# Even spacing of filler blocks in the seven-product pairs, a tied convolution product, and two transposes set a step apart, in a Mamba-2 layer

## The chip, the cores and the metric

The kernel runs on one core of a Trainium2 chip. The metric is the device time of one execution in microseconds, taken over several executions, and the median is used. One further execution was recorded by the hardware profiler; every duration, wait and clock below is from that one.

Engine names: PE is the matrix engine, DVE the vector engine, ACT the scalar engine, POOL the general engine, SP the engine that issues most DMAs.

## The reference

Four steps are chained on a residual stream of 256 tokens by 2048 columns in fp32: multi-head latent attention, a squared-ReLU MLP, a Mamba-2 mixer, a second MLP. Only the Mamba-2 mixer is touched here:

```python
def ssm_mixer(h, w_in, conv_w, conv_b, dt_bias, a_log, d_skip, norm_g, w_out):
    zxbcdt = h @ w_in                            # 2048 -> 4096 z, 4096 x, 1024 B, 1024 C, 64 dt
    z, xbc, dt = jnp.split(zxbcdt, [...], axis=-1)
    xbc = jax.nn.silu(causal_depthwise_conv(xbc, conv_w, conv_b))     # 4 taps along the tokens
    ...
    y = ssd_chunked_scan(xs, dt, a, b_in, c_in)  # 64 heads in 8 groups
    y = y + d_skip[..., None] * xs
    y = y.reshape(B, S, SSM_D_INNER) * jax.nn.silu(z)
    y = y.reshape(B, S, SSM_GROUPS, 512)
    y = y * lax.rsqrt(jnp.mean(y * y, axis=-1, keepdims=True) + RMS_EPS)
    return (y.reshape(B, S, SSM_D_INNER) * norm_g) @ w_out
```

## The kernel before

**Arithmetic.** Each fp32 operand is split into a high word that the PE takes at full rate and a remainder. A product of activations and weights is then three matmuls: high by high, low by high, high by low. Weights come in pieces of 128x1024 (512 KB), called units: one DMA into a raw buffer (`wraw`, or `wrx` where the unit needs a longer life), an ACT copy that gives the high word `wh` (L102), a DVE subtraction that gives the remainder `wl` (L103). `wh` and `wl` have four buffers each, so a unit can be split only when PE has used up the unit four before it. The raw buffers are a ring too: a load starts when the last reader of the buffer before it is done.

**Stage.** The touched stage lies between about 1018 and 1526 us. It first makes B and C (columns "B 0" and "C 0"), the dt chain, and block x4; then the x columns of groups 0 to 3 in two *pairs*, p0 and p1, of two groups each; then a list of steps `SSM_ORDER`: convolutions ("v"), the second halves of B and C, z blocks ("z", with the gating of y) and output blocks ("o").

**A pair** computes a 2x2 block product by seven products instead of eight (`ssm_seven`). The products are M1, N7, N5, N6, N4, M2, N3, each cut into four depths d = 0..3. A piece is written here as N70 (product N7, depth 0): six matmuls, 1.36 us on PE. Some of them need weights that are sums of two quarters; DVE forms these in place (L183, `b22`, `b12` and `b11`): in front of N7 `b22 = b12 + b22`, in front of N5 `b12 = b11 + b12`, in front of N6 `b11 = b11 + b22`. N4 uses `b11` again after a DMA has added a quarter to it.

**Fillers.** A product piece of 1.36 us on PE needs up to two DVE operations of 1.22 us, so PE would outrun DVE. Between the pieces therefore stand fillers: eighths of the x blocks of groups 5, 6 and 7 (x5/0 is the first eighth of x5), twelve matmuls, 2.72 us on PE, one DVE operation. `woven(p)` writes the order: it balances a sum of PE time against a sum of DVE time, with earliest times for N4, M2 and N3. `SSM_FILLERS` says which eighths belong to which pair. The order that it gives for the end of p0, the start of p1, and the end of p1:

```text
p0: ... N63 x6/3 M20 M21 M22 M23 N30 N31 N32 N43 N33
p1: x6/4 x6/5 M10 N70 x6/6 N50 x6/7 N60 M11 N71 x7/0 N51 x7/1 N61 x7/2 N40 M12 N72 x7/3 N52 ...
p1: ... N53 x7/6 N63 x7/7 N42 M20 M21 M22 M23 N30 N31 N43 N32 N33
```

**Ticks.** Work beside the matmuls is put into a queue by `later(n, fn)`: it runs at the n-th coming tick. Outside the pairs every two units of a block (24 matmuls, 5.4 us) end with a tick; inside them `spend` counts 5.4 us of PE time as one.

**Order on the engines.** PE runs in program order. On the other engines a list scheduler sets the order when the kernel is built, except where `issue_after` ties an instruction behind another one: `behind("last_lo")` ties DVE work behind the remainder (L103) that was written last, `behind("last_load")` ties loads behind the last weight load on SP.

**Convolution of x** (`x_conv(g, wait)`). The x columns were written to DRAM (`put_x`, L1326 and L1327) and are read back four times, shifted by 0 to 3 tokens: `xtm` (L1353) and three `tap` tiles (L1344); each has its weights `cw` (L1340). DVE multiplies and adds them: `mult` takes the unshifted rows and tap 2, `tapped(1)` tap 1 (L1359 the product, L1356 the sum), `total` the rest. Group 0's is called in p1 when N5 and N6 are both complete (`free`, at N63).

**Gating of y** (`z_block(g)`). When y of group g is ready, `gate` makes for each token half t = 0, 1 a gated and normed 128x512 tile, and three ticks later `transposes` turns it on PE into a bank of PSUM (L322 and L324), which ACT and DVE then split into the k4 tiles that the output blocks read (L299, L300). The transposes use the pool `sm`, which has two banks. `cb_group` (L1307, L1308) uses the same pool, and its matmuls stand right ahead of the transposes at groups 3 and 4.

Of the kernel before, what the change touches and what calls it, by code (L numbers as in the profile page):

```python
# [214 lines left out]
class Trunk:  # L215
# [959 lines left out]
    def ssm_body(self, sp, dp, gain, later):  # L1175
# [15 lines left out]
        hq, cms, ready, gated, batch, sp2 = [], [], {}, set(), [], []  # L1191
# [143 lines left out]
        def x_conv(g, wait):  # L1335
            cw, tap, xts = {}, {}, []

            def weight(k):
                cw[k] = sp.tile([P, 512], F32, tag="cw", name=f"cw{g}_{k}", bufs=3)
                nc.sync.dma_start(cw[k], d["cwx"][g][:, k * 512:(k + 1) * 512])  # L1340

            def load(k):
                tap[k] = self.flow.pools["rx"].tile([P, 2, 512], F32, tag="rx", name=f"tap{g}_{k}")
                nc.sync.dma_start(tap[k], x_rows(g, 0, 2, k))  # L1344

            def fetch(*todo):
                with behind("last_load"):
                    for fn in todo:
                        fn()

            def whole():
                xts.append(xn.tile([P, 2, 512], F32, tag="xn", name=f"xtm{g}"))
                nc.sync.dma_start(xts[0], x_rows(g, 0, 2))  # L1353

            both = lambda k: cw[k].unsqueeze(1).to_broadcast([P, 2, 512])
            plus = lambda v: nc.vector.tensor_tensor(xts[0], xts[0], v, ALU.add)  # L1356

            def tapped(k):
                nc.vector.tensor_tensor(tap[k], tap[k], both(k), ALU.mult)  # L1359
                plus(tap[k])  # L1360

            def mult():
                with behind("last_lo"):
                    nc.vector.tensor_tensor(xts[0], xts[0], both(3), ALU.mult)
                    tapped(2)
                fetch(lambda: weight(0), lambda: weight(4))

            def total():
                with behind("last_lo"):
                    plus(both(4))  # L1370
                    tapped(0)

            def tanh():
                tap[3] = self.flow.pools["rx"].tile([P, 2, 512], F32, tag="rx", name=f"th{g}")
                with behind("last"):
                    nc.scalar.activation(tap[3], xts[0], AF.Tanh, scale=0.5)

            def silu():
                with behind("last_lo"):
                    nc.vector.scalar_tensor_tensor(xts[0], tap[3], 1.0, xts[0], ALU.add, ALU.mult)  # L1380

            def ahead():
                x = xg[g] = [xts[0][:, t] for t in range(2)]
                heads_of = lambda v: v.rearrange("p (h f) -> p h f", h=8)
                spread = lambda v: v[:, 8 * g:8 * g + 8].unsqueeze(2).to_broadcast([P, 8, 64])
                xw = self.scratch()
                nc.gpsimd.tensor_tensor(heads_of(xw), heads_of(x[0]), spread(edge[:, 0]), ALU.mult)

                def across():
                    b = self.bank(False)  # L1390
                    nc.tensor.matmul(b, cb[g][:, P:256], xw, start=True, stop=True)
                    far[g] = sp2[0].tile([P, 512], F32, tag="far", name=f"far{g}", bufs=2)
                    nc.vector.tensor_tensor(heads_of(far[g]), heads_of(b), spread(edge[:, 1]), ALU.mult)

                self.later(2, across)

            self.later(wait, lambda: fetch(whole, lambda: weight(3), lambda: load(2), lambda: weight(2), lambda: load(1)))
            self.later(wait + 1, lambda: fetch(lambda: weight(1), lambda: load(0)))
            self.later(wait + 3, mult)
            self.later(wait + 4, lambda: tapped(1))  # L1400
            self.later(wait + 4, lambda: cb_group(g))
            self.later(wait + 5, lambda: (total(), hq.extend((g, i) for i in range(8))))
            self.later(wait + 6, tanh)
            self.later(wait + 7, lambda: (silu(), ahead()))
# [61 lines left out]
        yT = [None] * GROUPS  # L1466

        def z_block(g):
            accs = self.block([("si", "z", g, q) for q in range(4)], xT)
            ssq = self.stat(2)  # L1470
            ws = []
            for t in range(2):
                w = self.scratch()
                nc.scalar.activation(w, accs[t], AF.Tanh, scale=rsh[t])
                nc.vector.scalar_tensor_tensor(w, w, 1.0, accs[t], ALU.add, ALU.mult)
                ws.append(w)
            yT[g] = (self.ktile(self.k4), self.ktile(self.k4))

            def gate():
                if self.ticks < ready.get(g, self.ticks + 1):  # L1480
                    self.later(0, gate)
                    return
                ng = self.gain_tile(d["sng"][g], nc.gpsimd)
                for t in range(2):
                    x = xg[g][t]
                    nc.gpsimd.tensor_tensor(x, ws[t], x, ALU.mult)
                    self.square_sum(x, ssq[:, t:t + 1], scale=rs[t])
                rr = self.rsqrt(ssq, 2, 512, 4 * EPS)
                r = self.stat(2)
                nc.vector.tensor_tensor(r, rr, rs2, ALU.mult)  # L1490
                for t in range(2):
                    nc.vector.scalar_tensor_tensor(ws[t], xg[g][t], r[:, t:t + 1], ng, ALU.mult, ALU.mult)
                    w = self.words(ws[t], 4 - t)
                    self.later(3, lambda t=t, w=w: self.transposes(w, yT[g][0], yT[g][1], t, False))
                self.later(3, lambda: gated.add(g))

            self.later(0, gate)

# [4 lines left out]
        out = {}  # L1503
# [12 lines left out]
        with ExitStack() as first:  # L1516
            sp1 = first.enter_context(self.tc.tile_pool(name="ssm1", bufs=1, reuse_waits="tile"))
            sums, steps = self.sums_of_tokens(sp1, xn)
            for n, fn in zip(SUMS_AT, steps):
                self.later(n, fn)  # L1520
            bc_block("B", 0)
            dt_block()
            bc_block("C", 0)
            x_block(4)
            for p in range(2):
                self.ssm_seven(sums, p, filler, lambda p, j, t, src, dst: put_x(2 * p + j, t, src, dst),
                               (lambda: x_conv(0, 0)) if p else None)
        sp2.append(later.enter_context(self.tc.tile_pool(name="ssm2", bufs=1, reuse_waits="tile")))
        self.pump = pump

        for step in SSM_ORDER:
# [12 lines left out]
            else:  # L1544
# [12 lines left out]
HEAD_BACKLOG = 4  # L1557
TINY = 1.2e-38
SUMS_AT = (5, 8, 11)
SSM_FILLERS = [[("x", 5, o) for o in range(8)] + [("x", 6, o) for o in range(4)],  # L1560
               [("x", 6, o) for o in range(4, 8)] + [("x", 7, o) for o in range(8)]]
SSM_ORDER = ["v1+3", "B1", "C1", "v2+1", "z0", "z1", "v3", "z2", "z3", "v4", "o0a", "o0b", "v5", "z4", "z5", "v6", "o1a", "v7+1",
             "o1b", "z6", "z7", "o2a", "o2b", "o3"]

# [1 line left out]
def woven(p):  # L1566


    main = [(n, d) for d in range(4) for n in ("M1", "N7", "N5", "N6")]
    late = [("N4", d) for d in range(4)]  # L1570
    second = [("M2", d) for d in range(4)] + [("N3", d) for d in range(4)]
    units = list(SSM_FILLERS[p])
    pe = 28 * 1.36 + 2.72 * len(units)
    ve = 40 * 1.22 + 1.22 * len(units) + 5 * 0.68
    t = work = 0.0
    rest, done, out = -9.0, {}, []

    def ready(n, d):
        if n == "N4":
            return t >= done.get(("N6", d), 1e9) + 12  # L1580
        if n == "M2":
            return t >= done.get(("M1", 3), 1e9) + 7
        if n == "N3":
            return t >= max(done.get((q, 3), 1e9) for q in ("N5", "N6")) + 7
        return True

    while main or late or second or units:
        op = next((q for q in (late, main, second) if q and ready(*q[0])), None)
        if units and t >= rest and (op is None or work > t * ve / pe - 2):
            b = units.pop(0)  # L1590
            out.append(b)
            t, work = t + 2.72, work + 1.22
            if b[2] == 7:
                rest = t + 4
        else:
            if op is None:
                op = late or second
            n, d = op.pop(0)
            out.append(("s", p, n, d))
            t, work = t + 1.36, work + {"M1": 1.22, "N4": 1.22, "M2": 1.22, "N3": 1.22}.get(n, 2.44)  # L1600
            done[n, d] = t
    return out

# [220 lines left out]
```

## Time and profile before

| | |
|---|---|
| median of 3 runs | 2300.14 us (2298.83 to 2300.56) |
| the profiled execution | 2302.01 us, its span 2300.2 us, mean granted clock 0.997 |
| PE busy | 2277.0 us, 99% of the span |
| DVE, ACT, POOL busy | 1961.4 (85%), 1443.1 (63%), 279.7 us (12%) |
| the stage, 1022 to 1180 us (both pairs) | PE busy 149.8 of 158 us |
| the stage, 1180 to 1526 us | PE busy 340.3 of 346 us |
| PE's waits from 1010 to 1530 us | 8.1 us for `wl`, 4.7 us for a bank at L322, 0.9 us elsewhere |

The profiled execution is 1.9 us above the median, and 1.8 us of it lie around the span. A line of the timeline reads: start and duration in us, engine, line, operation, what it writes and reads, shapes, count, and in brackets how long the engine stood idle before it and what it waited for. A line of the waits reads: who waits, for whom, us in total, times, longest. In a table of windows each engine has its busy time and number of instructions, then come the granted clock of PE (1.00 is full speed), the DMA engines' share, and GB/s. A matmul's printed duration overlaps the next one's, so distances between starts are what count.

### The profile page before, as it was taken

The numbers are of one execution on the slowest core, as the hardware profiler recorded it, in microseconds if no ns is written. First come the engines' busy times: TensorE is split into PE (matmuls) and PEld (weight loads), VectorE is DVE, ScalarE is ACT, GpSimd is POOL, SyncE is SP. The second block draws the span as 40 slices with busy tenths as digits, with TensorE's granted clock in tenths as the row PEclk, the third lists the DMA queues.
The fourth block names the chain that finished last, engine by engine and source line by source line (L and its number), as shares of the span: only waits on it lengthen the run. The fifth ranks groups of instructions, "written<-read, shape, count | busy, mean of one in ns | idle before, by whom it ended". The sixth has DMA issues, their size and how long they took to land.

```text
span 2300.2 us, 30834 instructions
## 1 busy us (share of the span) xinstructions
PE 2277.0 (99%) x10881; PEld 1884.4 (82%) x10881; DVE 1961.4 (85%) x2257; ACT 1443.1 (63%) x2044; POOL 279.7 (12%) x339
## 2 busy tenths in 40 slices
PE   9999999999999999999999999999999999999999
PEld 7888888888888888888778887788888887888887
DVE  7786698998899897887879998876989989989985
ACT  7775466566666666566567676564666665666663
POOL 1440000000000000100002532230000000000000
PEclk9999999999999999999999999999999999999999
DMA  8545688888888877768798888866688888888875
GB/s 314 171 153 166 210 232 265 257 257 258 271 256 258 275 226 244 246 186 274 231 340 289 285 284 295 303 213 221 204 260 247 266 268 247 257 271 250 264 230 164
DMA packets 176026, 569.74 MB, mean 248 GB/s; under 512 B 20192, under 2 KB 29344, under 8 KB 175872
## 3 DMA queue, kind: packets, MB, share of 16 engines
q1 hardware_dynamic: 147808, 498.24, 65.0%
q0 software_dynamic: 16320, 56.88, 11.6%
q10 hardware_dynamic: 11744, 12.66, 1.7%
q8 instruction: 85, 1.39, 0.2%
q14 instruction: 69, 0.57, 0.1%
HBM read 542.23 MB, written 6.41 MB: 239 GB/s over the span
## 4 chain that ended last, share of the span: by engine, by line
PE 89%; DVE 5%; DMA 3%; ACT 1%; issue 1%; POOL 0%; ACTq 0%; DVEq 0%; SPq 0%
PE acc L339 10%; PE acc L340 10%; PE acc L343 10%; PE yp L619 9%; PE yp L618 9%; PE yp L617 9%; PE st L618 7%; PE st L619 7%; PE st L617 7%; DVE wl L103 3%; DMA wraw<-mi 1%; PE st L1162 1%; PE yp L339 1%; PE yp L340 1%; PE yp L343 1%
## 5 line engine op out<-in xcount | busy, mean ns | idle before, releaser
L102 ACT ACTIVATE wh<-wraw 128x1024 fp32r<-128x1024 f32 (+1 forms) x818 | 857.8, 1053 | 541.6 <-PE acc L340 189.9
L103 DVE TENSOR_TENSOR wl<-wraw,wh 128x1024 fp32r<-128x1024 f32 (+1 forms) x818 | 986.1, 1224 | 171.4 <-ACT wh L102 162.6
L617 PE MATMUL yp<-wh,k 128*128 128x512 f32 x896 | 349.3, 390 | 0.0
L619 PE MATMUL yp<-wh,k 128*128 128x512 f32 x896 | 348.8, 389 | 0.0
L618 PE MATMUL yp<-wl,k 128*128 128x512 f32 x896 | 348.6, 389 | 0.0
L102 ACT ACTIVATE wh<-wrx 128x1024 fp32r<-128x1024 f32 x192 | 203.0, 1059 | 169.5 <-PE yp L619 98.4
L103 DVE TENSOR_TENSOR wl<-wrx,wh 128x1024 fp32r<-128x1024 f32 x192 | 233.0, 1221 | 39.8 <-ACT wh L102 39.2
L339 PE MATMUL acc<-wh,k 128*128 128x512 f32 x496 | 196.7, 397 | 0.3 <-ACT k L299 0.3
L618 PEld LDWEIGHTS yp<-wl,k 128*128 128x128 f32 x896 | 168.2, 188 | 35.0
L619 PEld LDWEIGHTS yp<-wh,k 128*128 128x128 f32 x896 | 168.2, 188 | 34.9
L617 PEld LDWEIGHTS yp<-wh,k 128*128 128x128 f32 x896 | 168.3, 188 | 34.8
L340 PE MATMUL acc<-wh,k 128*128 128x512 f32 x496 | 193.7, 391 | 0.8 <-DVE k L300 0.8
L339 PE MATMUL acc<-wh,xt 128*128 128x512 f32 x480 | 191.5, 399 | 0.3 <-ACT wh L102 0.2
L340 PE MATMUL acc<-wh,xt 128*128 128x512 f32 x480 | 187.6, 391 | 0.1
L617 PE MATMUL st<-wh,xt 128*128 128x512 f32 x448 | 177.7, 397 | 0.0
L619 PE MATMUL st<-wh,xt 128*128 128x512 f32 x448 | 174.9, 390 | 0.0
L618 PE MATMUL st<-wl,xt 128*128 128x512 f32 x448 | 174.7, 390 | 0.0
L199 POOL DMA_DIRECT2D wrx<-mi x56 | 49.0, 875 | 723.5 <-DVE wl L103 513.0
L617 PE MATMUL st<-wh,sN 128*128 128x512 f32 x336 | 133.1, 396 | 0.8 <-ACT wh L102 0.8
L618 PE MATMUL st<-wl,sN 128*128 128x512 f32 x336 | 131.5, 392 | 1.5 <-DVE wl L103 1.3
L343 PE MATMUL acc<-wl,k 128*128 128x512 f32 x496 | 132.7, 389 | 0.0
L619 PE MATMUL st<-wh,sN 128*128 128x512 f32 x336 | 131.1, 390 | 0.0
(342 smaller groups left out, 3811.1 us busy)
## 6 DMA issues: line engine op xcount, KB each, us to landing
wraw<-mi SPq DMA_DIRECT2D x256, 512.0 KB, 5.7
wraw<-mo SPq DMA_DIRECT2D x256, 512.0 KB, 5.4
wraw<-si SPq DMA_DIRECT2D x160, 512.0 KB, 5.6
wraw<-so SPq DMA_DIRECT2D x64, 512.0 KB, 4.8
wrx<-mi SPq DMA_DIRECT2D x56, 512.0 KB, 5.4
wrx<-mi POOLq DMA_DIRECT2D x56, 512.0 KB, 7.6
wraw<-wo SPq DMA_DIRECT2D x32, 512.0 KB, 3.9
tap<-xD SPq DMA_DIRECT2D x24, 512.0 KB, 8.5
```

What stands on the lines that cost most here:

```text
L102: self.last = nc.scalar.activation(h[:, v], raw[:, v], AF.Copy)
L103: self.last_lo = nc.vector.tensor_tensor(lo[:, v], raw[:, v], h[:, v].bitcast(F32), ALU.subtract)
L199: nc.gpsimd.dma_start(st["b11"].tile, quarter(d, 1, 0), accum_op=ALU.add)
L339: nc.tensor.matmul(accs[t][:, :n], ah, wh[:, q, :], start=first and kt + q == 0, stop=False)
L340: nc.tensor.matmul(accs[t][:, :n], al, wh[:, q, :], start=False, stop=False)
L343: nc.tensor.matmul(accs[t][:, :n], lhs(kt + q, t)[0], wl[:, q, :], start=False, stop=en and q == nk - 1)
L617: nc.tensor.matmul(b, ah, wh, start=first and q == 0, stop=False)
L618: nc.tensor.matmul(b, ah, wl, start=False, stop=False)
L619: nc.tensor.matmul(b, al, wh, start=False, stop=last and q == 1)
L1162: nc.tensor.matmul(bank[onto], ah, wl, start=False, stop=done == 3 and q == 1, skip_group_check=skip)
```

## The change

It has three parts. No instruction is added or taken away on any engine; outside this stage the order stays as it was.

1. `woven` places the fillers by count instead of by a balance of costs: two to begin with, the rest spread evenly over the 16 main pieces, and `SSM_TAIL` of them (3 in p0, 4 in p1) behind these, one after every three pieces. p0 now has 11 and p1 13. Since there are more pieces behind N63, group 0's convolution is asked for one tick later.
2. `tapped(1)` is tied behind the last remainder.
3. The transposes of t = 1, and the mark that the group is gated, come one tick later than those of t = 0, except at groups 1 and 7.

```diff
+            def some():
+                with behind("last_lo"):
+                    tapped(1)
...
-            self.later(wait + 4, lambda: tapped(1))
+            self.later(wait + 4, some)
...
+            apart = int(g not in (1, 7))
...
-                    self.later(3, lambda t=t, w=w: self.transposes(w, yT[g][0], yT[g][1], t, False))
-                self.later(3, lambda: gated.add(g))
+                    self.later(3 + t * apart, lambda t=t, w=w: self.transposes(w, yT[g][0], yT[g][1], t, False))
+                self.later(3 + apart, lambda: gated.add(g))
...
-                               (lambda: x_conv(0, 0)) if p else None)
+                               (lambda: x_conv(0, 1)) if p else None)
...
-SSM_FILLERS = [[("x", 5, o) for o in range(8)] + [("x", 6, o) for o in range(4)],
-               [("x", 6, o) for o in range(4, 8)] + [("x", 7, o) for o in range(8)]]
+SSM_FILLERS = [[("x", 5, o) for o in range(8)] + [("x", 6, o) for o in range(3)],
+               [("x", 6, o) for o in range(3, 8)] + [("x", 7, o) for o in range(8)]]
+SSM_TAIL = (3, 4)
...
-    pe = 28 * 1.36 + 2.72 * len(units)
-    ve = 40 * 1.22 + 1.22 * len(units) + 5 * 0.68
+    share = (len(units) - SSM_TAIL[p] - 2) / 18
...
-        if units and t >= rest and (op is None or work > t * ve / pe - 2):
+        if main:
+            filler = used < 2 + share * len(done)
+        else:
+            filler = run > 2
+        if units and (op is None or filler):
```

The new order at the same places:

```text
p0: ... N42 x6/0 M20 M21 M22 x6/1 M23 N43 N30 x6/2 N31 N32 N33
p1: x6/3 x6/4 M10 x6/5 N70 N50 x6/6 N60 M11 N71 x6/7 N51 N61 x7/0 M12 N40 N72 x7/1 N52 ...
p1: ... N53 N63 N42 x7/4 M20 M21 M22 x7/5 M23 N43 N30 x7/6 N31 N32 N33 x7/7
```

Three places on DVE, as the two kernels are built. A name carries the number of its unit (`wl485`), so equal numbers are not equal pieces in the two kernels.

First, DVE from the end of p0 into p1. Before: 483 is N32, 484 N43, 485 N33, 486 and 487 are x6/4 and x6/5, 488 is M10, and `wraw489` is b22 for N70.

```order
L103 TENSOR_TENSOR wl483_10023<-wraw483_9986,wh483_10022 128x1024
L103 TENSOR_TENSOR wl484_10037<-wrx469_9768,wh484_10036 128x1024
L183 TENSOR_TENSOR wraw489_10060<-wraw489_10058,wraw489_10060 128x1024
L103 TENSOR_TENSOR wl485_10049<-wraw485_10008,wh485_10048 128x1024
L103 TENSOR_TENSOR wl486_10063<-wraw486_10020,wh486_10062 128x1024
L103 TENSOR_TENSOR wl487_10075<-wraw487_10034,wh487_10074 128x1024
```

After: 483 is N32, 484 N33, 485 and 486 are x6/3 and x6/4, 487 is M10.

```order
L103 TENSOR_TENSOR wl483_10016<-wraw483_9966,wh483_10015 128x1024
L103 TENSOR_TENSOR wl484_10028<-wraw484_9984,wh484_10027 128x1024
L103 TENSOR_TENSOR wl485_10046<-wraw485_9998,wh485_10045 128x1024
L103 TENSOR_TENSOR wl486_10060<-wraw486_10013,wh486_10059 128x1024
L183 TENSOR_TENSOR wraw489_10057<-wraw489_10055,wraw489_10057 128x1024
L103 TENSOR_TENSOR wl487_10070<-wrx487_10025,wh487_10069 128x1024
```

The sum for N70 stood ahead of the remainders of N33 and of two fillers, and now stands behind all three.

Second, DVE in the middle of p1, around the sum b22 for N73. Before: 500 is x7/2, 501 N40, 502 M12, 503 N72, and `wraw510` is b22 for N73; its load goes into the buffer that 500 frees.

```order
L103 TENSOR_TENSOR wl500_10281<-wraw500_10231,wh500_10280 128x1024
L183 TENSOR_TENSOR wraw503_10278<-wraw503_10276,wraw503_10278 128x1024
L103 TENSOR_TENSOR wl501_10293<-wrx488_10046,wh501_10292 128x1024
L183 TENSOR_TENSOR wraw503_10276<-wrx502_10256,wraw503_10276 128x1024
L103 TENSOR_TENSOR wl502_10309<-wrx502_10256,wh502_10308 128x1024
L183 TENSOR_TENSOR wraw510_10373<-wraw510_10371,wraw510_10373 128x1024
L103 TENSOR_TENSOR wl503_10322<-wraw503_10278,wh503_10321 128x1024
```

After: 498 is x7/0, 499 M12, 500 N40, 501 N72, and `wraw508` is b22 for N73; its load goes into the buffer that 498 frees.

```order
L103 TENSOR_TENSOR wl498_10237<-wraw498_10195,wh498_10236 128x1024
L183 TENSOR_TENSOR wraw501_10232<-wrx499_10207,wraw501_10232 128x1024
L103 TENSOR_TENSOR wl499_10261<-wrx499_10207,wh499_10260 128x1024
L183 TENSOR_TENSOR wrx499_10207<-wrx499_10207,wraw501_10234 128x1024
L183 TENSOR_TENSOR wraw508_10339<-wraw508_10337,wraw508_10339 128x1024
L103 TENSOR_TENSOR wl500_10271<-wrx487_10025,wh500_10270 128x1024
L103 TENSOR_TENSOR wl501_10284<-wraw501_10234,wh501_10283 128x1024
```

Before, four rows lay between the freeing remainder and the sum, N40's and M12's remainders among them; now three rows do, and N40's and N72's remainders stand behind the sum.

Third, DVE at the tap product of group 0. Before: 519 is M22, 520 M23, 521 and 522 are N30 and N31, 523 is N43.

```order
L103 TENSOR_TENSOR wl519_10576<-wraw519_10501,wh519_10575 128x1024
L1359 TENSOR_TENSOR tap0_1_10547<-tap0_1_10547,cw0_1_10595 128x1024
L103 TENSOR_TENSOR wl520_10586<-wraw520_10519,wh520_10585 128x1024
L103 TENSOR_TENSOR wl521_10602<-wraw521_10549,wh521_10601 128x1024
L103 TENSOR_TENSOR wl522_10614<-wraw522_10573,wh522_10613 128x1024
```

After: 529 and 530 belong to block B1, the first of `SSM_ORDER` behind the pairs.

```order
L103 TENSOR_TENSOR wl529_10719<-wraw529_10652,wh529_10718 128x1024
L103 TENSOR_TENSOR wl530_10737<-wraw530_10664,wh530_10736 128x1024
L1359 TENSOR_TENSOR tap0_1_10557<-tap0_1_10557,cw0_1_10606 128x1024
L1311 SCALAR_TENSOR_TENSOR cb0_10757<-sm_795_10754,tri_8827 128x128
L1356 TENSOR_TENSOR xtm0_10549<-xtm0_10549,tap0_1_10557 128x1024
```

The product stood inside the pair, ahead of M23's remainder; now it stands behind the fifth unit of the block that follows the pair.

On SP the group's first five loads stood ahead of the weight loads of N30 and N31 before, and stand ahead of those of N32 and N33 now. On PE the three transposes L322 and the one L324 of t = 1 stood right behind those of t = 0; now the next 24 matmuls of a block stand between them, at groups 3 and 4 also the 64 products L1447.

More of the change, by code (lines that the diff above doesn't have):

```diff
@@ L1572, in woven @@
     units = list(SSM_FILLERS[p])
-    pe = 28 * 1.36 + 2.72 * len(units)
-    ve = 40 * 1.22 + 1.22 * len(units) + 5 * 0.68
-    t = work = 0.0
-    rest, done, out = -9.0, {}, []
+    share = (len(units) - SSM_TAIL[p] - 2) / 18
+    t, used, run, done, out = 0.0, 0, 0, {}, []
     def ready(n, d):
@@ L1588, in woven @@
         op = next((q for q in (late, main, second) if q and ready(*q[0])), None)
-        if units and t >= rest and (op is None or work > t * ve / pe - 2):
[L1590 to L1594, printed above, removed]
+        if main:
[3 more added lines that the diff above has]
+        if units and (op is None or filler):
+            out.append(units.pop(0))
+            t, used, run = t + 2.72, used + 1, 0
         else:
@@ L1599, in woven @@
             out.append(("s", p, n, d))
-            t, work = t + 1.36, work + {"M1": 1.22, "N4": 1.22, "M2": 1.22, "N3": 1.22}.get(n, 2.44)
+            t, run = t + 1.36, run + 1
             done[n, d] = t
```

## The prediction

> **What bounds the kernel now.** I read the page's busy times first, then the chain that ended last, then the waits of PE inside the stage that the change touches (1010 to 1530 us).
>
> ```profile
> PE 2277.0 (99%) x10881; PEld 1884.4 (82%) x10881; DVE 1961.4 (85%) x2257; ACT 1443.1 (63%) x2044; POOL 279.7 (12%) x339
> PE 89%; DVE 5%; DMA 3%; ACT 1%; issue 1%; POOL 0%; ACTq 0%; DVEq 0%; SPq 0%
> ...
> PE st L1162 <- DVE wl L103: 8.1, 3, 5.3
> PE sm L322 <- DVE k L300: 4.7, 2, 3.1
> ```
>
> PE is the bound, and only its idle time and its half-speed time can be won. In the stage it waits 8.1 us for remainders (wl, the third matmul of a product at L1162), 4.7 us for a transpose bank (L322), and under 1 us elsewhere. PE's timeline shows each place and where matmuls regain their spacing; the chain shows the spacing.
>
> ```profile
> 1096.12 0.79 PE L1162 MATMUL st<-wl,sN 128*128 128x512 f32 x1 [2.63 <-DVE wl L103]
> 1102.75 0.40 PE L339 MATMUL yp<-wh,xt 128*128 128x512 f32 x1
> ...
> 1168.81 0.80 PE L1162 MATMUL st<-wl,xt 128*128 128x512 f32 x1 [5.34 <-DVE wl L103]
> 1174.05 0.40 PE L1162 MATMUL st<-wl,sN 128*128 128x512 f32 x1
> ...
> 1407.58 0.45 PE L322 MATMUL sm<-ident,tr 128*128 128x128 f32 x3 [3.14 <-DVE k L300]
> 1457.36 0.45 PE L322 MATMUL sm<-ident,tr 128*128 128x128 f32 x3 [1.58 <-DVE k L300]
> ```
>
> ```profile
> 1173.44 0.43 PE st L1160
> ...
> 1174.22 0.23 PE st L1162
> 1174.45 0.23 PE st L1160
> ```
>
> A matmul comes every 0.23 us (0.227 over long stretches), so a product of six is 1.36 us and a filler of twelve 2.72 us. After both waits for wl it comes every 0.43 us for a while. Between 1096.12 and 1102.75 stand 16 matmuls: 6.63 us instead of 3.63, 3.0 us lost. Between 1168.81 and 1174.05 stand 12: 5.24 instead of 2.72, 2.5 us lost. The windows show that the granted clock does it, and that the 3.14 us at L322 did not.
>
> ```profile
> 1095.00:1100.00 5.00, 3.88 (x9) 3.11 (x10) 5.00 (x6) 1.78 (x2) 0.00 (x0) 0.55 0.63 209
> 1170.00:1175.00 5.00, 5.00 (x16) 3.90 (x15) 3.38 (x3) 2.74 (x4) 0.00 (x0) 0.60 0.81 229
> ...
> 1404.00:1408.00 4.00, 0.86 (x10) 0.68 (x8) 4.00 (x7) 0.60 (x1) 0.00 (x0) 1.00 0.55 167
> ```
>
> What DVE did before the two late remainders:
>
> ```profile
> 1093.70 1.23 DVE L183 TENSOR_TENSOR wraw<-wraw,wraw 128x1024 f32<-128x1024 f32 x1 [3.17 <-DMA wraw<-si]
> 1094.84 3.49 DVE L103 TENSOR_TENSOR wl<-wraw,wh 128x1024 fp32r<-128x1024 f32 x3
> ...
> 1166.39 1.22 DVE L1359 TENSOR_TENSOR tap<-tap,cw 128x1024 f32<-128x1024 f32 x1 [7.21 <-DMA cw<-cwx]
> 1167.54 2.35 DVE L103 TENSOR_TENSOR wl<-wraw,wh 128x1024 fp32r<-128x1024 f32 x2
> ```
>
> First: pair 1's sum b22 of N70 (L183) waits for its load and holds up the remainder of N33 of pair 0 behind it. Second: group 0's tap 1 (L1359) waits 7.21 us for its weights and holds up M23 of pair 1.
>
> **The change, part by part.** No instruction is added or removed on any engine; all of it is order.
>
> *Fillers, end of pair 0.* The sum of N70 moves behind the remainders of N33, x6/3 and x6/4. When it waits, PE still has N32, N33 and two fillers, 8.2 us; the wait of 3.17 and two DVE rows of 1.14 are 5.4 us. Cover holds: 2.63 + 3.0 = 5.6 us won (if the load came 3 us later, the cover would be gone).
>
> *Tap 1 and the end of pair 1.* The tap product moves behind a remainder of block B1, past the end of the pair. Its weights took 12.28 us; issued behind those of x7/7, some 17 us before the pair's end, they land some 5 us before it, and the product stands some 5 us behind it: no wait there. Won: 5.34 + 2.5 = 7.8 us. But the tap was not the only late thing:
>
> ```profile
> 1154.02 12.28 DMA cw<-cwx
> ...
> 1147.41 0.39 SPq L1353 DMA_DIRECT2D xtm<-xD  x1
> ...
> 1150.84 2.09 SPq L85 DMA_DIRECT2D wraw<-si  x2
> ...
> 1163.87 1.06 ACT L102 ACTIVATE wh<-wraw 128x1024 fp32r<-128x1024 f32 x1 [1.95 <-DMA wraw<-si]
> 1165.35 1.06 ACT L102 ACTIVATE wh<-wraw 128x1024 fp32r<-128x1024 f32 x1 [0.43 <-DMA wraw<-si]
> ```
>
> From 1147.41 SP issues group 0's five conv loads (2 MB) and behind them the weights of N30 and N31, which land 13 us after their issue. With `x_conv(0, 1)` the burst goes one tick later and stands ahead of the weights of N32 and N33. PE then has ten products and four fillers behind N63, 24.5 us, where it had 16.3. Counted back from the end of pair 1: N63 ends at -24.5, the remainder of M21 frees the last slot ahead of the burst at -22.6, the burst takes 3.4 us of SP, so N32's weights are issued at -18.9. At 12.9 us they land at -6.0, and hi and remainder (1.06 + 1.22) are there at -3.7, where PE wants the remainder at -6.4: a stall of 2.7 us. The two 256 KB writes of block x7 now lie behind instead of in this traffic, some 1.2 us at the 410 GB/s that the windows of 1160 to 1170 show. I take 1.7 us, between 0 (landing in 10 us) and 2.9 (with N33 late too).
>
> ```profile
> 1160.00:1165.00 5.00, 3.47 (x16) 2.54 (x14) 0.00 (x0) 2.69 (x3) 0.00 (x0) 1.00 1.04 410
> ```
>
> *Fillers, middle of pair 1.* Here the new order makes a wait that was harmless into one that is not. DVE before:
>
> ```profile
> 1045.89 1.22 DVE L103 TENSOR_TENSOR wl<-wraw,wh 128x1024 fp32r<-128x1024 f32 x1
> 1053.56 1.23 DVE L183 TENSOR_TENSOR wraw<-wraw,wraw 128x1024 f32<-128x1024 f32 x1 [3.04 <-DMA wraw<-si]
> ...
> 1122.19 1.23 DVE L103 TENSOR_TENSOR wl<-wraw,wh 128x1024 fp32r<-128x1024 f32 x1 [0.62 <-ACT wh L102]
> 1123.34 1.22 DVE L183 TENSOR_TENSOR wraw<-wraw,wraw 128x1024 f32<-128x1024 f32 x1
> 1124.47 1.22 DVE L103 TENSOR_TENSOR wl<-wrx,wh 128x1024 fp32r<-128x1024 f32 x1
> 1125.61 1.22 DVE L183 TENSOR_TENSOR wraw<-wrx,wraw 128x1024 f32<-128x1024 f32 x1
> 1126.74 1.22 DVE L103 TENSOR_TENSOR wl<-wrx,wh 128x1024 fp32r<-128x1024 f32 x1
> 1130.84 1.23 DVE L183 TENSOR_TENSOR wraw<-wraw,wraw 128x1024 f32<-128x1024 f32 x1 [2.88 <-DMA wraw<-si]
> ```
>
> The last row is b22 of N73. The remainder at 1122.19 frees the slot that its load goes into; from the end of that remainder to the sum it is 7.4 us (6.4 at 1053.56). N40 and M12 were converted in between, so PE had work. In the new order the slot is freed by x7/0, only three DVE rows ahead of the sum, and N40 and N72 stand behind it. With 0 at PE's start of M10 of pair 1 and unstalled PE, N40's third matmul is due at 23.6. DVE's sum of N70 starts at about -5.0 (its slot is freed at -12.0, plus 7); 20 rows of 1.14 us, one of 0.6 among them, and 0.4 of waiting end x7/0's remainder at 17.6; plus 6.4 to 7.4 the sum of N73 starts at 24.0 to 25.0, and N40's remainder ends 2.4 later, at 26.4 to 27.4. Stall: 2.8 to 3.8, and I take 3.4. With DVE abreast of PE and the page's median landing it would be 0; with 9 us, 5.
>
> ```profile
> wraw<-si SPq DMA_DIRECT2D x160, 512.0 KB, 5.6
> ...
>   DMA wraw<-si: 10.3, 5
> ```
>
> *Clock.* Of four idle stretches, 2.63 and 5.34 halved it, 3.14 and 1.58 did not. So I give the new 3.4 an even chance and the 1.7 one in four: none 0.37, one 0.5, both 0.13. One halving costs 2.75, the mean of 3.0 and 2.5; I take one.
>
> The Trainium skill (TensorE: Matmul & The Clock Gate, HAM oscillation) warns only of idle gaps beyond about 3.4 us. By it the two new stalls would leave the clock alone and the sum would lack the 2.75; the trace disagrees, since 2.63 us was enough.
>
> *Transposes of gated y.* t=1 needs the bank that t=0 has just filled, whose eviction stood behind other work in DVE's queue (the chain at group 3):
>
> ```profile
> 1405.39 1.13 DVE xtm L1356
> 1406.52 0.40 DVE cb L1311 x2
> 1406.92 0.61 DVE k L300
> ```
>
>  One step later puts 24 matmuls (5.4 us) between, at groups 3 and 4 the 64 small products too: more than 3.14 and 1.58. Won: 4.7 us. The o blocks that read the result stand a further block behind. At groups 0, 2, 5 and 6 nothing waited: nothing won or lost. No DMA and nothing of POOL moves.
>
> **Sum.** 5.6 + 7.8 + 4.7 = 18.1 won; 3.4 + 1.7 + 2.75 = 7.85 lost: 10.3 less. The profiled run took 2302.0, its span 2300.2, so the span should come to 2289.9; against the median of 2300.14 that is 2289.8 us.
>
> **The rivals.**
> - *The clock stays up*, or only one of the two stalls comes: 13.1 to 15 won, 2285 to 2287. For it: 3.14 us without a halving. Against: the two stalls of this kind both had one.
> - *No new stall*: 18.1 won, 2282. For it: the 5.6 us landing; against: five of the pairs' sums waited for loads, 10.3 us together (the last row above), three of them 2.9 to 3.2. The Trainium skill (DMA: Bandwidth & Descriptors, the fit of time by bytes) makes 512 KB an estimated 3.2 us; by it neither load would be late and this case would hold, but the trace has twice as much and more.
> - *Both stalls halve the clock, or one is at its upper end*: 5 to 9 won, 2291 to 2295.
> - *The end of pair 1 is not mended*: tap 1 was only the later of two, and the weights behind the burst hold PE nearly as long. Then 7.8 is lost from the gain: 18.1 - 7.8 - 6.15 = 4.2, within 0.2% (4.6 us, about what a measurement here can tell), 2296.
> - *Slower*: spread fillers put a load-bound sum ahead of the next remainder at every depth, not at one. Each such place costs 3.0 + 2.75 = 5.75; there are eight sums in the pairs. At three the gain is gone, from four it is over 0.2% slower (2305), at five 2311. For it: those five waits. Against: only one of them reached PE.
>
> **How the numbers follow.** Forecast 0.36; clock up or one stall 0.22; no stall 0.10; both halved 0.17; end of pair 1 not mended 0.10; slower 0.05. The first four are faster by over 0.2%: 0.85. The range of 2282 to 2295 holds them but for their edges.
>
> **What would show it.** Right: no wait at L1162 near the old 1096 and 1168; L322 gone from PE's waits; a new wait of L1162 on wl of about 3 us some 25 us into pair 1, DVE's sum of N73 waiting 3 to 4 us for its load ahead of it; a second one at N32, with ACT waiting for wraw. Wrong: PE without idle time in pair 1, or waits at N7 sums in pair 0, where I found about 1 us of slack and no stall.

## The result and the profile after

| | median (runs) | profiled run, its span |
|---|---|---|
| before | 2300.14 us (2295.97 to 2302.01, 7) | 2302.01, 2300.2 us |
| after | 2293.26 us (2290.66 to 2294.88, 7) | 2291.82, 2290.0 us |

The ratio is 0.9971, with a 95% interval of 0.9959 to 0.9983: 6.9 us faster by the medians. The span of the profiled run, 2290.0, stands almost on the 2289.9 of the sum, but that is in part luck: the two profiled runs lie 10.2 us apart, the medians only 6.9. And the experiments show that two of the three parts win nothing alone, and that the third wins more than the sum gave it.

PE's waits inside the stage, after. The whole list is two lines:

```profile
PE st L1162 <- DVE wl L103: 6.4, 1, 6.4
PE acc L343 <- DVE wl L103: 1.9, 1, 1.9
```

L322 is gone. The waits of 2.63 and 5.34 us at L1162 are gone too, and one wait of 6.4 us has come. PE's timeline, then DVE's, show its place:

```profile
1126.62 0.80 PE L1162 MATMUL st<-wl,xt 128*128 128x512 f32 x1 [6.37 <-DVE wl L103]
1127.22 0.63 PE L1160 MATMUL st<-wh,xt 128*128 128x512 f32 x1
...
1269.57 1.20 PE L343 MATMUL acc<-wl,xt 128*128 128x512 f32 x4 [1.90 <-DVE wl L103]
```

```profile
1113.86 1.22 DVE L103 TENSOR_TENSOR wl<-wraw,wh 128x1024 fp32r<-128x1024 f32 x1
1114.99 1.22 DVE L183 TENSOR_TENSOR wraw<-wrx,wraw 128x1024 f32<-128x1024 f32 x1
1116.13 1.22 DVE L103 TENSOR_TENSOR wl<-wrx,wh 128x1024 fp32r<-128x1024 f32 x1
1117.38 1.23 DVE L183 TENSOR_TENSOR wrx<-wrx,wraw 128x1024 f32<-128x1024 f32 x1
1124.21 1.23 DVE L183 TENSOR_TENSOR wraw<-wraw,wraw 128x1024 f32<-128x1024 f32 x1 [5.60 <-DMA wraw<-si]
1125.35 1.22 DVE L103 TENSOR_TENSOR wl<-wrx,wh 128x1024 fp32r<-128x1024 f32 x1
```

These are the rows of the second place in the order: x7/0, the sum for N52, M12, the sum for N62, then the sum b22 of N73, which idles 5.60 us for its load, and N40 behind it. The chain gives the load 9.01 us from the moment that x7/0 freed its buffer:

```profile
1115.10 9.01 DMA wraw<-si
```

The windows show that the clock was at half behind the wait, and that it is back soon:

```profile
1125.00:1130.00 5.00, 3.38 (x8) 2.70 (x9) 5.00 (x6) 1.06 (x1) 0.00 (x0) 0.50 0.24 55
1130.00:1135.00 5.00, 5.00 (x20) 4.01 (x20) 4.01 (x4) 2.12 (x2) 0.87 (x1) 0.86 0.82 253
```

At group 3 the transposes of t = 1 now come behind the 64 products (L1451, before L1447) and 24 matmuls, without a wait:

```profile
1398.66 0.53 PE L322 MATMUL sm<-ident,tr 128*128 128x128 f32 x4
1399.13 2.08 PE L1451 MATMUL y<-xtm,mt 128*64 128x64 f32 x64
1406.72 0.37 PE L322 MATMUL sm<-ident,tr 128*128 128x128 f32 x3
```

### The profile page after: what moved, and what is told of

It is laid out like the page before. It is cut to its first block, busy times and chain, and to the rows that moved or that the text cites. A ratio compares the mean times of both kernels' runs of the same rounds, so it can differ in the third digit from the quotient of the medians.

```text
span 2290.0 us, 30852 instructions
## 1 busy us (share of the span) xinstructions
PE 2271.9 (99%) x10881; PEld 1881.8 (82%) x10881; DVE 1964.8 (86%) x2257; ACT 1442.9 (63%) x2044; POOL 284.8 (12%) x339
## 4 chain that ended last, share of the span: by engine, by line
PE 90%; DVE 4%; DMA 3%; issue 1%; ACT 1%; POOL 0%; ACTq 0%; SPq 0%; DVEq 0%
PE acc L339 10%; PE acc L340 10%; PE acc L343 10%; PE yp L618 9%; PE yp L619 9%; PE yp L617 9%; PE st L618 7%; PE st L619 7%; PE st L617 7%; DVE wl L103 2%; DMA wraw<-mi 1%; PE st L1162 1%; PE st L1160 1%; PE st L1161 1%; DMA wraw<-si 1%
## 5 line engine op out<-in xcount | busy, mean ns | idle before, releaser
L619 PE MATMUL st<-wh,xt 128*128 128x512 f32 x448 | 174.9, 390 | 0.0
L343 PE MATMUL acc<-wl,k 128*128 128x512 f32 x496 | 132.7, 389 | 0.0
```

What stands on the lines that cost most here:

```text
L343: nc.tensor.matmul(accs[t][:, :n], lhs(kt + q, t)[0], wl[:, q, :], start=False, stop=en and q == nk - 1)
L619: nc.tensor.matmul(b, al, wh, start=False, stop=last and q == 1)
```

## Experiments

Three stretches of PE's timeline, whose ends are the same matmul in every kernel, show where each kernel spends the stage: the *pairs* (M10 of p0 to the first matmul of B1), the *middle* (to `cb_group` of group 4), the *gates* (to the first product of the last y). One profiled run each, in us; the ratios are from all runs. The two kernels with less work compute only a part of the convolution:

| kernel | pairs | middle | gates | ratio to before, 95% |
|---|---|---|---|---|
| before | 151.4 | 175.8 | 181.0 | |
| spacing alone (e1) | 145.8 | 180.2 | 183.6 | 1.0001 (0.9992 to 1.0011) |
| tie alone (e2) | 148.1 | 176.6 | 185.7 | 1.0000 (0.9990 to 1.0009) |
| transposes alone (e3) | 147.8 | 174.9 | 176.0 | 0.9973 (0.9962 to 0.9984) |
| spacing and tie (e9) | 146.9 | 177.1 | 186.1 | 1.0012 (1.0002 to 1.0021) |
| spacing and transposes (e10) | 144.9 | 179.8 | 176.0 | 0.9976 (0.9967 to 0.9985) |
| tie and transposes (e11) | 146.0 | 176.2 | 176.0 | 0.9956 (0.9941 to 0.9970) |
| all three: after | 145.5 | 176.6 | 176.0 | 0.9971 (0.9959 to 0.9983) |
| after, sums tied (e4) | 142.6 | 180.8 | 176.0 | 0.9955 (0.9939 to 0.9972) |
| e4, less DVE work (e6) | 142.0 | 177.3 | 176.0 | 0.9933 (0.9913 to 0.9953) |
| e4, less DMA (e7) | 138.9 | 176.6 | 176.0 | 0.9927 (0.9911 to 0.9943) |
| e4, group 2 a tick later (e8_v2_2) | 140.2 | 179.2 | 178.6 | 0.9952 (0.9934 to 0.9971) |
| e4, group 2 two ticks later (e8_v2_3) | 140.5 | 177.3 | 182.0 | 0.9957 (0.9941 to 0.9973) |
| tie, transposes, sums tied (e12) | 139.5 | 176.1 | 176.0 | 0.9938 (0.9923 to 0.9952) |

Without waits the pairs are 600 matmuls of 0.227 us, 136 us. The pairs of one order vary from run to run: before and e3 have the same instructions there and 151.4 and 147.8 us. The mean granted clock, which is on record for every run, says how the other runs fared (0.001 of it is 2.3 us): on average 0.996 in e1 and e9, 0.997 in before and e2, 0.998 in e3, e10 and the change, 0.999 in e4 and e11, 1.000 in e12.

### Each part alone

The spacing alone is the change with `apart = 0` and

```diff
-            self.later(wait + 4, some)
+            self.later(wait + 4, lambda: tapped(1))
```

> Only the even spacing of the fillers (with the conv called one tick later); tap 1 untied, both transposes in one step. Theory (the 6.4 us wait for N73's sum is the price of the spacing; the tie adds nothing at group 0, because the later call alone already puts tap 1 behind N33's remainder; the gates are worth 4.7 us): PE waits 6 to 7 us once for wl at L1162 near 1120 us, 3.1 and 1.6 us at L322, none at M23; wait at L343 near 1270 us back at about 0.7; span 2293 to 2295 us. Rival (the tie is what mended M23): a wait of 3 us or more at the end of pair 1, span 2297 or more.

Measured: 2300.24 us (2299.36 to 2302.85, 10 runs), span 2301.1. PE's waits:

```profile
PE st L1162 <- DVE wl L103: 6.6, 2, 5.6
PE sm L322 <- DVE k L300: 5.1, 2, 3.6
PE acc L343 <- DVE wl L103: 2.9, 1, 2.9
PE sm L1220 <- DVE far L1393: 1.4, 1, 1.4
```

The waits in the pairs and at L322 are where the theory put them, and M23 has none: the later call had already moved tap 1 out of the pair's way. But the gain that the theory counted on (a span of 2293 to 2295) is not there; the span lies in the rival's range, without the rival's wait. The pairs are 5.6 us shorter, and the middle is 4.4 longer: 1.4 us at L1220 and 2.9 near 1273 us, both for DVE, the second with half speed behind it. The gates cost 2.6 us more than before.

The tie alone is before with `some` as in the change.

> Only tap 1 tied behind the last remainder. Theory (the tap was only the later of two late things at M23: the weights of N30 and N31 stand behind the conv loads and come 13 us after their issue): the 5.3 us wait at M23 becomes one of 1.5 to 3 us at N30, the waits of 2.6 and of L322 stay; gain 2 to 5 us, span 2295 to 2298. Rival (the tap alone was late): no wait left at the end of pair 1, gain 7.8 us, span 2292.4.

Measured: 2300.77 us (2298.72 to 2304.01, 10 runs), span 2301.7. PE's waits:

```profile
PE sm L322 <- DVE k L300: 6.5, 2, 4.0
PE st L1162 <- DVE wl L103: 6.1, 4, 3.0
```

The waits at the end of pair 1 are 0.5 to 0.6 us each, so both mechanism and size of my theory failed there: the weights behind the burst came almost in time. Yet no time was won, against theory and rival: the wait at N33 of p0 was 3.0 us in this run, one of 2.1 came earlier, and the two waits at L322 were 4.0 and 2.5 us. Half speed followed each of these four.

The transposes alone are before with the two `later` lines of the gate as in the change.

> Only the transposes of t = 1 a step later. Theory: L322 leaves PE's waits, all others stay, gain 4.7 us, span 2295.5. Rival (the eviction of the bank only moves on to the next reader): an equal wait at L339 or L343 behind it, gain under 1 us, span 2299 to 2300.

Measured: 2294.05 us (2291.67 to 2295.90, 7 runs), span 2292.4. PE's waits:

```profile
PE st L1162 <- DVE wl L103: 7.2, 4, 4.8
PE acc L343 <- DVE wl L103: 0.2, 1, 0.2
```

This part alone is as fast as the whole change, 6 us and not 4.7. The gates explain most of it: with the transposes apart they take 176.0 us in every kernel of the table but the two that move group 2's convolution, in one step 181.0, 183.6, 185.7 and 186.1.

### Pairs of parts

> The changed kernel without the third part: both transposes in one step again. Theory (the transposes are worth 4.7 us of waiting and often a stretch of half speed; spacing and tie together win 6 us in the pairs and give 1 to 2 back behind them): waits at L322 of 3 to 4 and 1.5 to 2.5 us, pairs of 145 to 146 us, span 2295 to 2297. Rival (spacing and tie are worth nothing together, as alone): span 2299 to 2301.

Measured: 2302.43 us (2300.93 to 2304.52, 10 runs), span 2299.2. The rival was nearer: no gain, even 0.1% slower. The gates of this run show what a longer wait at L322 does to the 64 products behind it, which took 2.08 us above:

```profile
1404.51 0.45 PE L322 MATMUL sm<-ident,tr 128*128 128x128 f32 x3 [4.24 <-DVE k L300]
1404.80 0.30 PE L324 MATMUL sm<-ident,s 128*128 128x128 f32 x1
1405.02 3.25 PE L1451 MATMUL y<-xtm,mt 128*64 128x64 f32 x64
```

> The changed kernel without the second part: tap 1 of every group untied. Theory (untied, the products of tap 1 wait some 3 us for their weights behind the pairs, ahead of the remainders, in a stretch in which DVE has no time to spare): pairs as in the changed kernel, a wait near 1270 of 2.5 to 3.5 us for wl instead of 1.9, span 2292 to 2294. Rival (the tie does nothing): wait of 1.9, span 2290.

Measured: 2294.36 us (2293.22 to 2297.62, 10 runs), span 2292.6. As the theory said, DVE waits behind the pairs for the weights of a tap (group 1's, at 1206 us), and PE waits 3.0 us near 1270 where it was 1.9:

```profile
DVE tap L1359 <- DMA cw<-cwx: 3.2, 1, 3.2
...
PE acc L343 <- DVE wl L103: 3.0, 1, 3.0
```

> The changed kernel without the first part: the old order of the fillers, tap 1 tied, transposes a step apart. Theory (spacing wins little net, since what it wins in the pairs is asked back behind them): span 2291 to 2294, median within 2 us of that of the whole change. Rival (spacing carries the change): span 2295 or more.

Measured: 2290.01 us (2288.86 to 2291.23, 4 runs), span 2288.1. Without the spacing the kernel is no slower but, at the medians, 3 us faster than with it; the intervals overlap. It is also 4 us faster than the transposes alone (e3): all four runs lie below all seven of e3 (2291.67 at least), though the intervals of the ratios overlap by a little. So the tie, which won nothing by itself, seems to win once the transposes are apart.

### The wait at N40, and what the middle asks back

In this kernel b22 of N71, N72 and N73 in the two pairs is tied behind the last remainder:

```diff
             if name == "N7":
-                add("b22", "b12", "b22")
+                with flow.tc.issue_after(flow.last_lo.ins) if len(prefix) == 1 and d else nullcontext():
+                    add("b22", "b12", "b22")
```

> The changed kernel with one more edit: in the two pairs the sums b22 for N71, N72 and N73 are tied behind the last remainder in program order, so that N73's waits for its load behind N40 and not ahead of it. Theory: the wait of 6.4 us and the half-speed time behind it (2.0 us) go, span 2281 to 2283. Rival (the load is the limit and not the place of the sum): PE waits as long at N72 or N73, span 2288 to 2290.

Measured: 2291.05 us (2288.99 to 2292.82, 4 runs), span 2291.0. PE's waits (lines moved: L344 is L343 of before, L1164 is L1162, and L1162 is L1160):

```profile
PE acc L344 <- DVE wl L103: 4.3, 2, 3.2
PE st L1162 <- ACT wh L102: 1.2, 2, 0.9
PE st L1164 <- DVE wl L103: 1.2, 3, 0.5
```

The 6.4 us are gone, so it was the place of the sum, as the prediction had it. But the span misses the ranges of theory and rival alike, and hardly more than 2 us were won at the medians, with overlapping intervals. The pairs are only 2.9 us shorter in these two runs, since a dozen waits of 0.9 us and less have come, half of them too short to be listed. The middle is 4.2 us longer, with 4.3 us of waits near 1265 instead of 1.9 and half speed behind the longer one. Two kernels take away what the middle could lack. Each leaves out or replaces a part of the convolution, and the second also takes no raw buffer for tap 1, so it frees more than the DMA engines.

```diff
             def some():
+                if g < 3:
+                    return
                 with behind("last_lo"):
                     tapped(1)
```

> The kernel with the tied sums, with the arithmetic of tap 1 left out for groups 0 to 2 (its product and its sum, six DVE operations of 1.22 us); its loads stay, so this leaves out a part of the convolution. Theory (behind the pairs DVE is the bound: it is busy 11 to 12 of every 12 us from 1205 to 1300, so time won in the pairs comes back as a wait for wl near 1270): the waits of 3.2 and 1.1 us near 1260 to 1270 and the half-speed time behind them go, 5 to 6 us less than with the tied sums, span 2285 to 2286. Rival (the DMA engines are the bound, at 93 to 105% from 1150 to 1215): the waits stay at 3.5 us or more, under 1 us won.

```diff
             def load(k):
+                if k == 1 and g < 3:
+                    tap[1] = tap[2]
+                    return
```

> The kernel with the tied sums, with tap 1 of groups 0 to 2 not loaded (1.5 MB less, 3.7 us of all DMA engines at 410 GB/s); its arithmetic stays and runs on tap 2's tile, so the convolution's second tap is replaced. Theory (DVE is the bound there): waits of 3.5 to 4.5 us for wl near 1260 to 1270 stay, span 2290 to 2292. Rival (DMA is the bound): they fall below 1.5 us, 3 to 6 us won, span 2285 to 2288.

Less DVE work: 2286.45 us (2284.68 to 2289.03, 4 runs), span 2286.1. Less DMA: 2285.07 us (2282.94 to 2286.60, 4 runs), span 2281.2. PE's waits near 1260 to 1270 in the first, then in the second:

```profile
PE acc L344 <- DVE wl L103: 1.2, 2, 0.9
```

```profile
PE acc L344 <- DVE wl L103: 1.8, 1, 1.8
```

Against e4 either helps by 5 to 6 us at the medians (the intervals of the ratios overlap), so neither theory alone holds. In the second 3.7 us of it lie in the pairs. The waits of the other engines from 1180 to 1270 fit one reading: in e4 and in the first kernel ACT waits 5.2 us for late weights, in the second it waits for none, and DVE's idle time for high words falls from 4.1 us in e4 to 2.3. DVE's lateness near 1270 would then be the sum of its work and of its idling for late loads, and the two kernels cut one each. This is argued and not shown, as the second kernel changes the buffers too.

Two more kernels only put work off: group 2's convolution one or two ticks later, on top of the tied sums (`"v2+1"` becomes `"v2+2"`, `"v2+3"`).

> The kernel with the tied sums, and the convolution of group 2 one tick later (v2+2 in place of v2+1). Theory (DVE is the bound near 1270 and some 9% idle after 1300): two operations of 1.22 us leave the queue ahead of the late remainder, so the wait falls from 3.2 to about 1 us, 2 to 4 us won, span 2287 to 2289. Rival (the work only moves ahead of the next remainders): as long a wait 5 to 10 us later, span 2290 to 2292.

> The same with group 2's convolution two ticks later (v2+3). Theory: four to five operations leave the queue ahead of the late remainder, no wait near 1270, 4 to 6 us won, span 2285 to 2287. Rival (the work only moves): a wait of 3 us or more between 1275 and 1300, or group 2's scores come too late for its z block, span 2290 or more.

Measured: 2289.67 us (2288.61 to 2294.70, 4 runs), span 2288.3, and 2291.68 us (2290.53 to 2293.58, 4 runs), span 2288.9. The wait near 1270 fell to 0.5 us or less, and others took its place: 1.1 us at 1278 and 2.3 us at the transposes in the first, 1.6 us at 1301 and 3.3 us at 1369 in the second. The first span lies in the theory's range, the second in neither, and by the medians neither kernel differs from e4 beyond the error. The work moved, as the rivals said, but further than they said.

### The old spacing with tied sums

> The old order of the fillers, with tap 1 tied, transposes a step apart, and the sums b22 of all N7 pieces tied behind the last remainder. Theory (the late remainders come from load-bound work that the scheduler put ahead of them, and tying does what the spacing did): no wait of over 1 us in the pairs but some 1 to 2 us at N30, whose weights stand behind the conv loads; pairs of 138 to 142 us; a wait near 1270 of 3 us or more; span 2288 to 2291. Rival (the spacing is needed for DVE to keep up): waits for wl of 2 us or more in the middle of a pair, pairs of 144 us or more, span 2292 or more.

It is e11 with the `issue_after` of above for every d. Measured: 2285.70 us (2283.84 to 2288.35, 4 runs), span 2282.1, ratio 0.9938 (0.9923 to 0.9952). It beats before and after, and its span lies below the theory's range: the wait near 1270, given as 3 us or more, is half as long. PE's waits in the stage:

```profile
PE acc L344 <- DVE wl L103: 1.5, 1, 1.5
PE st L1164 <- DVE wl L103: 1.1, 3, 0.5
PE st L1162 <- ACT wh L102: 0.5, 1, 0.5
```

The pairs take 139.5 us, shorter than with the spacing and the same ties, and the middle waits only 1.5 us for DVE where e4's waits 4.3. So the middle does not ask back whatever the pairs win: here they are 11.9 us shorter than before, and the middle is 0.3 us longer. The longer middles go with the spacing. Windows of the 10 us before and behind the start of B1, in e12 and then in e4:

```profile
1157.31:1167.31 10.00, 8.30 (x32) 5.24 (x30) 7.22 (x7) 6.71 (x8) 0.00 (x0) 1.00 1.03 395
1167.31:1177.31 10.00, 10.00 (x47) 8.32 (x46) 9.66 (x10) 7.63 (x12) 0.00 (x0) 1.00 0.99 359
```

```profile
1160.56:1170.56 10.00, 8.44 (x34) 5.71 (x32) 4.29 (x5) 4.86 (x6) 0.00 (x0) 1.00 1.03 380
1170.56:1180.56 10.00, 10.00 (x45) 8.29 (x46) 7.69 (x8) 6.66 (x8) 0.00 (x0) 1.00 0.94 331
```

In both the DMA engines are full. With the spacing DVE (the third pair of numbers) works 4.3 and 7.7 us of 10, without it 7.2 and 9.7. SP issues the five conv loads 22.6 us ahead of B1 in e4 and 26.1 in e12, so in e4 the crush of loads falls later, and DVE enters the middle with less done. That the later burst is the cause is argued from these rows; the spacing with the old call `x_conv(0, 0)` was not tried, and e12 also ties the sum of N70, which e4 leaves free.

## Why the prediction was right, and where it was wrong

The direction and the range (2282 to 2295) hold. Of the 10.3 us forecast, 6.9 came. Step by step:

- **End of pair 0, 5.6 us.** Right: with the spacing no kernel waits there for more than 1 us. The same was to be had by tying the sum (e12).
- **Tap 1, 7.8 us.** Right that the wait goes. But the edit named for it was not needed for it: e1 has no tie and no wait there either. Either the later call or the tie (e2) is enough.
- **N32 behind the burst, -1.7 us.** Mis-sized: PE loses nothing there. ACT does wait for late weights at the end of pair 1, three times, but each comes early enough:

```profile
ACT wh L102 <- DMA wraw<-si: 5.6, 3, 3.1
...
1156.29 2.97 SPq L85 DMA_DIRECT2D wraw<-si  x3
...
1164.88 1.06 ACT L102 ACTIVATE wh<-wraw 128x1024 fp32r<-128x1024 f32 x1 [2.07 <-DMA wraw<-si]
```

  N32's weights, the first of the three behind the burst, were there 8.6 us after their issue, where the sum had 12.9. The sum also had two slips. By the order that it used, N32, N33 and x7/7 are the last 24 matmuls, so N32's remainder is wanted at -5.0 us and not at -6.4, which is N31's time; and -22.6 plus 3.4 is -19.2. With both set right the stall is 1.0 us, less than the 1.2 that it took off for the writes.

- **N40 behind the sum of N73, -3.4 us.** The place, the mechanism and the three rows between were as forecast, and e4 shows it by removal. The size was 6.4, above my upper end of 5: the load took 9.0 us where I had 6.4 to 7.4 from two older rows, and DVE came later, since the sum of N70 started 3.7 us ahead of M10 (1092.45 against 1096.11 us) and not 5.0, so that x7/0's remainder ended at 19.0 us and not at 17.6.
- **Clock, -2.75 us.** Once, as taken, at 2.3 us by the same count (eleven distances of 4.84 us together instead of 2.50).
- **Transposes, 4.7 us.** Mis-sized. I counted the two waits of one profile and noted that 3.14 us had not halved the clock. In e1, e2 and e9 the first was 3.6 to 4.2 us and did, and in e2 and e9 the second, 2.5 us, did too. The gates cost 5.0 to 10.1 us more in one step than apart.
- **The sum.** This step failed. It took time won in the pairs for time won at the end. Net I gave spacing and tie 5.6 us; they bring no gain alone (e1, e2, e9), and against the transposes alone (e3) the whole change is 0.8 us faster at the medians, within the error. In the profiled run of the change the pairs were indeed 6.0 us shorter than before, but the pairs of before vary (147.8 us in e3), and the middle took 0.8 to 5.0 us longer than before in the kernels with the spacing that compute the whole. With the transposes in one step the gates asked for more as well: 2.6 to 5.1 us over before in e1, e2 and e9. I never priced the stretch behind the pairs, where the trace of before already showed a wait for wl at L343, and DVE (the third pair of numbers) busy 111 of the 120 us from 1180 on:

```profile
PE acc L343 <- DVE wl L103: 0.7, 1, 0.7
1180.00:1300.00 120.00, 119.27 (x647) 97.96 (x646) 110.98 (x129) 89.06 (x176) 37.48 (x20) 1.00 0.88 299
```

In e12, with the old spacing, the pairs are shorter still and the middle gives nearly all of it through; so the spacing was to be charged for its middle, and not every gain in the pairs.

So the errors cancel: the transposes won more than I gave them and the charge at N32 did not come, against too small a charge at N40 and none for the middle. That the sum came within 3.5 us of the measured median is therefore luck as much as insight. No rival had the third part carry the whole gain.

## What to carry to other kernels

Before a wait on the critical engine is removed, look at the next stretch: if another engine is busy there for over 90% of the time and a small wait for it shows already, as here, part of the gain can be asked back. Here that went with the spacing and not with e12's ties, which showed only when the edits were made alone and in pairs. A DVE instruction that waits for its load was here better tied behind the work that PE needs next than outrun by spacing: e12 has the old spacing, the shortest pairs of all kernels that compute the whole, and the best time. A wait of 3 us that left the clock alone in one profile is no evidence that it always does.

## What the runs showed of the hardware

Over all profiled kernels of this study PE stood idle in the stage for more than 2.5 us nineteen times. Eighteen times the matmuls behind it ran at half speed for a while (0.43 us apart, or the 64 products in 2.5 to 3.7 instead of 2.1 us), once (3.14 us, before) not. Of gaps between 2.0 and 2.5 us one of four did (2.07 us in e2; the same 2.07 us in e3 did not). The Trainium skill (TensorE: Matmul & The Clock Gate, HAM oscillation) draws the line at about 3.4 us; here half speed came mostly from 2.5 us on, and without a sharp line, since 2.07 us was enough once and 3.14 us was not.

In the clock records of these traces each of the nineteen stretches of half speed in the stage lasts 3.41 us (eleven) or 6.83 us (eight). The length of the wait alone does not say which: 6.83 us came with a wait of 2.63 us (before), 3.41 us with one of 4.0 us (e2).

A load of 512 KB into a buffer just freed took 6.4 to 9.0 us until DVE could use it in the middle of the pairs. Right behind the five conv loads the weights landed 12.6 us after their issue in before, and 8.5 to 8.9 us after it in the change. Why they came sooner there is open.
